# Value products of the samples' attention, ordered by page and turning over the four column quarters, in a two-layer decoder step

## The chip, the core and the metric

The kernel runs on one core of a Trainium2 chip. The metric is the device time of one execution in microseconds, as the median of the runs shown. TensorE multiplies and writes into PSUM, VectorE and ScalarE do elementwise work and empty PSUM, GpSimd (POOL) does elementwise work on SBUF and issues gathering DMAs, SyncE (SP) issues the other DMAs. Each engine works off its own queue in order, and semaphores tie the queues together.

## What is computed

The reference is one inference step of two decoder layers for a prompt of 512 tokens and for 8 samples, each with one new token and a paged cache of 2048 positions. A layer is a half-step FFN, a mixer and another half-step FFN, each with a LayerNorm. The mixer joins a state-space scan, a sparse attention and a short convolution. Only the sparse attention matters here. For a sample it has three branches (compressed keys, selected pages, window), each with its own softmax:

```python
s_c = einsum('btkgd,bnkd->btkgn', qg, kc);  o_c = softmax(s_c) @ vc          # 127 compressed positions
idx = top_k(score_from(p_c), 16)                                             # blocks of 64 positions
s_s = einsum('btkgd,btknsd->btkgns', qg, ks_sel);  o_s = softmax(s_s) @ vs_sel
s_w = einsum('btkgd,bwkd->btkgw', qg, kw);  o_w = softmax(s_w) @ vw          # last 512 positions
o = g[..., 0:1] * o_c + g[..., 1:2] * o_s + g[..., 2:3] * o_w
```

For the prompt the same three branches run over the 512 prompt tokens themselves. The compressed keys and values of a sample come from its whole cache by a small two-layer network (`nsa_compress`).

## The kernel before, in words

The products are 32-bit. The large ones are split into a high and a low half and run as three fast products; the small ones of the samples' attention run as plain 32-bit products, of which the profile shows each as two records (two weight loads, two matmuls).

The middle part of a layer (`mid`) has these stages. First, projections, and the fetch of the pages of the first group. Then `compress_cache`, a generator over the 8 samples: for each, eight steps of `prepare` (ScalarE and VectorE, L693 and L694, convert a slice of the 16 cache pages into two halves; the pages stand in tile cx or raw) and `products` (TensorE, L708, twelve matmuls), and then `second` (L736, L740). The pages of the next sample are fetched at the start of a sample (`fetch_cmp`, 16 DMAs on SP). `samples(l, g, ...)` is the attention of two samples, group g of four. Groups 0, 1 and 2 are woven with the compression of the next two samples, group 3 with `prompt_attention`, whose scores and values are L1048 to L1050, the transposes at L1060 and the values at L1071.

`weave` sets the order in which the two streams are written down: each stream yields the time that its last piece should cost, and the stream whose time has come goes next. So the numbers in `yield` are planned costs, in nanoseconds; a scheduler and the pools then place the instructions by engine.

In a group, z is the half of the pages (0 or 1) and j the sample (0 or 1). Page tile `G[z, j]` holds eight pages of keys (columns 0 to 127) and values (128 to 255) of one sample, in tile sg. Rows 64z + 32j to 64z + 32j + 31 of an output bank belong to (z, j): these 32 output rows are one column quarter of TensorE's array, so there are four quarters. `PT` holds the transposed probabilities, 128 columns for each of the eight page steps c and two window steps; `sT`, `srows` hold the new token's part (8 rows), `pc`, `vc` the compressed part (127 rows).

The value products at L1246 go through the quarters one by one: eight page steps of one quarter, with `fetch_sel` for that page tile of the next group behind them; for z = 0 the new token's product (L1250); a yield; two window steps (L1254); for z = 0 the new token's window product (L1257) and the compressed part (L1258). `fetch_sel` puts three gathering DMAs on POOL (L1111) and five DMAs on SP (L1115) for each page tile; they wait until the tile's value products have been read. `fetch_win` (L1120) loads two window tiles. Then three VectorE operations (L1262 to L1264) scale and add the branches, and L1266 sums on TensorE.

Of the kernel before, what the change touches and what calls it, by code (L numbers as in the profile page):

```python
# [122 lines left out]
class Trunk:  # L123
# [999 lines left out]
    def samples(self, l, g, p, pg, pw):  # L1123

        nc = self.nc
        G = self.sgq[g]
        QB, kcT, vc = self.QB, self.kcT, self.vc
# [18 lines left out]
        pc = p.tile([127, 64], F32, name="pc")  # L1146
# [3 lines left out]
        for k in range(4):  # L1150
            nc.tensor.matmul(M[:33, 196 + 33 * k:229 + 33 * k], pt[:, k:k + 1].to_broadcast([127, 33]), self.C["map"][:127],
                             start=True, stop=True)
        s, t = (p.tile([33, 4, 33], F32, name=n) for n in ("score", "rk"))
# [3 lines left out]
        own = p.tile([33, 4, 1], F32, name="own")  # L1157
# [17 lines left out]

        SB = p.tile([128, 1282], F32, name="SB")
        nc.vector.memset(SB[64:128, 0::1281], BIG)
        for c in range(2):
            S = self.bank(self.saS)
            for z in range(2):  # L1180
                for j in range(2):
                    r = 64 * z + 32 * j
                    nc.tensor.matmul(S[r:r + 32].rearrange("p (n t) -> p n t", n=4), QB[:, 2 * g + j], G[z, j][:, 4 * c:4 * c + 4, 0:128],
                                     start=True, stop=True)
                yield 1700.0, 0.0
            nc.vector.tensor_tensor(SB[:, 1 + 512 * c:513 + 512 * c].rearrange("p (n t) -> p n t", n=8), S.rearrange("p (n t) -> p n t", n=8),
                                    msk[:, 8 * c:8 * c + 8, None].to_broadcast([128, 8, 64]), op=OP.add)
        S = self.bank(self.saS)
        for j in range(2):
            for z in range(2):  # L1190
                r = 64 * z + 32 * j
# [26 lines left out]
        PT = p.tile([128, 10, 128], F32, name="PT")  # L1218
        for c0, n in ((0, 4), (4, 4), (8, 2)):
            T = self.bank(self.saT)  # L1220
            for c in range(n):
                o = 1 + 128 * (c0 + c)
                nc.tensor.transpose(T[:, c * 128:c * 128 + 128], SB[:, o:o + 128], self.ident)
            o, t = PT[:, c0:c0 + n].rearrange("p c r -> p (c r)"), T[:, :128 * n]
# [8 lines left out]
        sT = p.tile([NS, 128], F32, name="sT")  # L1233
# [4 lines left out]
        yield 300.0  # L1238

        O = self.bank(self.saS)  # L1240
        for z in range(2):
            for j in range(2):
                r = slice(64 * z + 32 * j, 64 * z + 32 * j + 32)
                own = slice(32 * j, 32 * j + 32)
                for c in range(8):
                    nc.tensor.matmul(O[r, :128], PT[:, c, r], G[z, j][:, c, 128:256], start=c == 0, stop=z == 1 and c == 7)  # L1246
                if g < 3:
                    self.fetch_sel(l, pg, g + 1, ((z, j),))
                if z == 0:
                    nc.tensor.matmul(O[r, :128], sT[:, own], self.srows[:, 128:256], start=False, stop=True)  # L1250
                yield 1900.0
                for c in range(2):
                    v = 512 + 256 * z + 128 * c
                    nc.tensor.matmul(O[r, 128:256], PT[:, 8 + c, r], G["w", j][:, v:v + 128], start=c == 0, stop=z == 1 and c == 1)  # L1254
                if z == 0:
                    o = slice(64 + 32 * j, 96 + 32 * j)
                    nc.tensor.matmul(O[r, 128:256], sT[:, o], self.srows[:, 384:512], start=False, stop=True)  # L1257
                    nc.tensor.matmul(O[r, 256:384], pc[:, own], vc[:127, j], start=True, stop=True)  # L1258
        if g < 3:
            self.fetch_win(l, pw, g + 1)  # L1260
        OS = p.tile([128, 128], F32, name="OS")
# [5 lines left out]
        for kv in range(2):  # L1267
            r = slice(kv * 64, kv * 64 + 64)
# [679 lines left out]
```

## Time and profile before

| | us |
|---|---|
| median of 3 runs | 3145.73 |
| lowest, highest | 3144.55, 3149.37 |
| profiled execution | 3151.41 |
| span of its trace, first to last instruction | 3149.70 |
| TensorE busy in it | 3078.8 |
| mean granted TensorE clock | 0.987 |

Terms of the sum are read from the one profiled execution, whose own time is 5.68 us above the median. In its trace the two layers repeat each other: the groups' value products begin at 555.7, 600.0, 648.9 and 703.3 us in the first layer. Busy time of TensorE counts a matmul to its modelled end, also where the next has begun, so differences of start times say more than durations.

### The profile page before, as it was taken

How to read it: one execution, taken by the hardware profiler on the slowest of the kernel's cores; microseconds unless marked ns; L12 is line 12 of the kernel's file. 1: busy time of each engine (PE TensorE's matmuls, PEld its weight loads, DVE VectorE, ACT ScalarE, POOL GpSimd, SP SyncE). 2: the span in 40 equal slices, each digit the busy share in tenths (PEclk: the TensorE clock that was granted, in tenths of full speed). 3: DMA queues.
4: the chain of work that ended last, by engine and by line, in shares of the span. 5: the costliest groups of instructions: out<-in, count | busy, mean ns of one | idle time of the engine just before them, and what ended most of it. 6: DMA issues, size and time to landing. Idle time of an engine off the chain costs nothing. (4 is left out here: it accounts for less than half of the span.)

```text
span 3149.7 us, 62116 instructions
## 1 busy us (share of the span) xinstructions
PE 3078.8 (98%) x25364; PEld 2949.6 (94%) x25364; DVE 1599.2 (51%) x3586; ACT 1121.1 (36%) x2226; POOL 531.5 (17%) x809
## 2 busy tenths in 40 slices
PE   8999999999999999999999999899999999999998
PEld 8999998877999999999999999888779999999998
DVE  7633356466655365333486334564566553653343
ACT  3332235455234233332233222254562242333322
POOL 2611031221001012001147110212210010210010
PEclk9999999999999999999999999899999999999999
DMA  5543254621543322223234332546215532322321
GB/s 156 202 149 133 89 152 136 205 81 29 173 131 106 96 86 96 93 82 100 76 117 170 99 101 83 162 123 213 68 54 165 136 105 81 108 81 85 104 84 65
DMA packets 358631, 360.18 MB, mean 114 GB/s; under 512 B 40069, under 2 KB 341669, under 8 KB 358217
## 3 DMA queue, kind: packets, MB, share of 16 engines
q1 hardware_dynamic: 342584, 333.58, 33.9%
q0 software_dynamic: 7440, 20.00, 2.2%
q8 instruction: 199, 3.26, 0.4%
q10 hardware_dynamic: 8320, 2.62, 0.4%
q14 instruction: 88, 0.71, 0.1%
HBM read 332.48 MB, written 36.28 MB: 117 GB/s over the span
## 5 line engine op out<-in xcount | busy, mean ns | idle before, releaser
L239 PE MATMUL ps<-xh,whi 128*128 128x264 f32 (+1 forms) x4448 | 1257.5, 285 | 15.3 <-ACT whi L228 7.8
L240 PE MATMUL ps<-xl,whi 128*128 128x264 f32 (+1 forms) x4448 | 1258.8, 284 | 2.0 <-DVE xl L323 2.0
L241 PE MATMUL ps<-xh,wlo 128*128 128x264 f32 (+1 forms) x4448 | 1255.5, 284 | 2.4 <-DVE wlo L229 2.4
L229 DVE TENSOR_TENSOR wlo<-raw,whi 128x1024 fp32r<-128x1024 f32 (+3 forms) x432 | 495.8, 1150 | 750.4 <-ACT whi L228 746.5
L239 PEld LDWEIGHTS ps<-xh,whi 128*128 128x128 f32 x4448 | 837.0, 189 | 20.1 <-ACT whi L228 8.8
L240 PEld LDWEIGHTS ps<-xl,whi 128*128 128x128 f32 x4448 | 840.1, 189 | 3.6 <-DVE xl L323 2.2
L241 PEld LDWEIGHTS ps<-xh,wlo 128*128 128x128 f32 x4448 | 839.6, 189 | 4.2 <-DVE wlo L229 3.6
L228 ACT ACTIVATE whi<-raw 128x1024 fp32r<-128x1024 f32 (+2 forms) x452 | 444.4, 988 | 892.2 <-PE ps L240 782.3
L240 PE MATMUL ps<-hl,whi 128*128 128x256 f32 (+1 forms) x1408 | 398.3, 283 | 0.0
L239 PE MATMUL ps<-hh,whi 128*128 128x256 f32 (+1 forms) x1408 | 398.2, 283 | 0.0
L241 PE MATMUL ps<-hh,wlo 128*128 128x256 f32 (+1 forms) x1408 | 398.1, 283 | 0.0
L241 PEld LDWEIGHTS ps<-hh,wlo 128*128 128x128 f32 x1408 | 265.3, 188 | 0.2
L239 PEld LDWEIGHTS ps<-hh,whi 128*128 128x128 f32 x1408 | 264.9, 188 | 0.3
L240 PEld LDWEIGHTS ps<-hl,whi 128*128 128x128 f32 x1408 | 264.8, 188 | 0.1
L260 POOL TENSOR_TENSOR xf<-xf,shift 128x264 f32<-128x264 f32 (+1 forms) x84 | 79.4, 982 | 1027.2 <-ACT shift L257 1027.2
L384 DVE TENSOR_TENSOR s<-s,ps 128x264 f32<-128x264 f32 (+1 forms) x176 | 74.3, 424 | 275.2 <-PE ps L241 274.9
L708 PE MATMUL ps<-xc,whi 128*128 128x256 f32 (+1 forms) x1024 | 165.2, 295 | 0.0
L385 ACT ACTIVATE hh<-s 128x264 fp32r<-128x264 f32 (+1 forms) x176 | 72.7, 415 | 245.7 <-DVE s L384 245.6
L708 PEld LDWEIGHTS ps<-xc,whi 128*128 128x128 f32 x1024 | 140.1, 190 | 14.6 <-issue 8.5
L1111 POOL DMA_INDIRECT sg<-in_selT_dram,idx x96 | 92.5, 963 | 289.9 <-PE ps L1246 257.3
L382 ACT ACTIVATE s<-ps 128x264 f32<-128x264 f32 (+1 forms) x176 | 66.2, 379 | 128.2 <-PE ps L241 126.0
L386 DVE TENSOR_TENSOR hl<-s,hh 128x264 fp32r<-128x264 f32 (+1 forms) x176 | 76.6, 437 | 33.5 <-ACT hh L385 33.5
(472 smaller groups left out, 4316.7 us busy)
## 6 DMA issues: line engine op xcount, KB each, us to landing
raw<-in_ffn_w_gu_dram SPq DMA_DIRECT2D x86, 1024.0 KB
raw<-in_w_in_dram SPq DMA_DIRECT2D x38, 1024.0 KB
raw<-in_ffn_w_down_dram SPq DMA_DIRECT2D x32, 1024.0 KB
sg<-in_selT_dram SPq DMA_DIRECT2D x160, 128.0 KB
cx<-in_cmpT_dram SPq DMA_DIRECT2D x128, 128.0 KB
raw<-in_cmpT_dram SPq DMA_DIRECT2D x128, 128.0 KB
raw<-in_ffn_w_down_dram SPq DMA_DIRECT2D x16, 768.0 KB
W<-in_winT_dram SPq DMA_DIRECT2D x16, 512.0 KB
```

Source lines behind the costliest of these rows:

```text
L228: self.copy = self.nc.scalar.activation(hi, raw, AF.Copy)
L229: self.lo.tensor_sub(lo, raw, hi.bitcast(F32))
L239: nc.tensor.matmul(o, hi[:, k], rh, start=start and k == 0, stop=False)
L240: nc.tensor.matmul(o, hi[:, k], rl, start=False, stop=False)
L241: nc.tensor.matmul(o, lo[:, k], rh, start=False, stop=stop and k == nk - 1)
L260: nc.gpsimd.tensor_sub(self.xf[:, g, a:b], self.xf[:, g, a:b], sc[:, :n])
L382: nc.scalar.activation(s[:, :n], g, AF.Silu)
L384: nc.vector.tensor_mul(s[:, :n], s[:, :n], u)
L385: nc.scalar.activation(hh[:, j, a:b], s[:, :n], AF.Copy)
L386: nc.vector.tensor_sub(hl[:, j, a:b], s[:, :n], hh[:, j, a:b].bitcast(F32))
L708: nc.tensor.matmul(o, w[:, 2 * qq + q2, :], x[:, 2 * q2:2 * q2 + 2, z:z + n], start=not b and s < 2 and q2 + z + m == 0, stop=s > 5 and q2 ...
L1111: nc.gpsimd.indirect_dma_start(out=t[:, k], out_offset=None, in_=flat, in_offset=bass.IndirectOffsetOnAxis(ap=self.idx[:, l, b, z, k:k + 1 ...
```

## The change

The value products of a group are written in another order. The page steps c are now the outer loop, and inside a step the four quarters take turns; the two window steps likewise. After page steps 3 and 7 the generator yields. `fetch_sel` is called once, for all four page tiles, behind the last page step. The products of the new token and of the compressed part come last, for one sample and then the other. Since the parts of a quarter now share its bank without finishing one after the other, only the very first product in a quarter starts the sum anew, and the check of groups is switched off for these products. The score products keep their order of quarters and yield once for four products (2200 planned ns) in place of twice (1700 each).

```diff
+        quarters = [(z, j, slice(64 * z + 32 * j, 64 * z + 32 * j + 32)) for z in range(2) for j in range(2)]
         for c in range(2):
             S = self.bank(self.saS)
-            for z in range(2):
-                for j in range(2):
-                    r = 64 * z + 32 * j
-                    nc.tensor.matmul(S[r:r + 32].rearrange("p (n t) -> p n t", n=4), QB[:, 2 * g + j], G[z, j][:, 4 * c:4 * c + 4, 0:128],
-                                     start=True, stop=True)
-                yield 1700.0, 0.0
+            for z, j, r in quarters:
+                nc.tensor.matmul(S[r].rearrange("p (n t) -> p n t", n=4), QB[:, 2 * g + j], G[z, j][:, 4 * c:4 * c + 4, 0:128],
+                                 start=True, stop=True)
+            yield 2200.0, 0.0
...
         O = self.bank(self.saS)
-        for z in range(2):
-            for j in range(2):
-                r = slice(64 * z + 32 * j, 64 * z + 32 * j + 32)
-                own = slice(32 * j, 32 * j + 32)
-                for c in range(8):
-                    nc.tensor.matmul(O[r, :128], PT[:, c, r], G[z, j][:, c, 128:256], start=c == 0, stop=z == 1 and c == 7)
-                if g < 3:
-                    self.fetch_sel(l, pg, g + 1, ((z, j),))
-                if z == 0:
-                    nc.tensor.matmul(O[r, :128], sT[:, own], self.srows[:, 128:256], start=False, stop=True)
+        for c in range(8):
+            for z, j, r in quarters:
+                nc.tensor.matmul(O[r, :128], PT[:, c, r], G[z, j][:, c, 128:256], start=c == 0, stop=z == 1 and c == 7,
+                                 skip_group_check=True)
+            if c % 4 == 3:
                 yield 1900.0
-                for c in range(2):
-                    v = 512 + 256 * z + 128 * c
-                    nc.tensor.matmul(O[r, 128:256], PT[:, 8 + c, r], G["w", j][:, v:v + 128], start=c == 0, stop=z == 1 and c == 1)
-                if z == 0:
-                    o = slice(64 + 32 * j, 96 + 32 * j)
-                    nc.tensor.matmul(O[r, 128:256], sT[:, o], self.srows[:, 384:512], start=False, stop=True)
-                    nc.tensor.matmul(O[r, 256:384], pc[:, own], vc[:127, j], start=True, stop=True)
+        if g < 3:
+            self.fetch_sel(l, pg, g + 1)
+        for c in range(2):
+            for z, j, r in quarters:
+                v = 512 + 256 * z + 128 * c
+                nc.tensor.matmul(O[r, 128:256], PT[:, 8 + c, r], G["w", j][:, v:v + 128], start=False, stop=z == 1 and c == 1,
+                                 skip_group_check=True)
+        for j in range(2):
+            own, o = slice(32 * j, 32 * j + 32), slice(64 + 32 * j, 96 + 32 * j)
+            nc.tensor.matmul(O[own, :128], sT[:, own], self.srows[:, 128:256], start=False, stop=True, skip_group_check=True)
+            nc.tensor.matmul(O[own, 128:256], sT[:, o], self.srows[:, 384:512], start=False, stop=True, skip_group_check=True)
+            nc.tensor.matmul(O[own, 256:384], pc[:, own], vc[:127, j], start=False, stop=True, skip_group_check=True)
+        yield 900.0
```

On TensorE's queue, in the first group of the first layer, the value products stood like this before (sg_5104, sg_5124, sg_5144 and sg_5164 are the page tiles of the four quarters; x8 is eight products in a row):

```order
L1246 MATMUL ps_6737<-sg_5104,PT_6595 32x128 x8
L1250 MATMUL ps_6737<-srows_4762,sT_6716 32x128
L1254 MATMUL ps_6737<-W_5184,PT_6595 32x128 x2
L1257 MATMUL ps_6737<-srows_4762,sT_6716 32x128
L1258 MATMUL ps_6737<-vc_6088,pc_6427 32x128
L1246 MATMUL ps_6737<-sg_5124,PT_6595 32x128 x8
L1250 MATMUL ps_6737<-srows_4762,sT_6716 32x128
```

Now the same place begins as follows, and goes on so for 32 products:

```order
L1242 MATMUL ps_6737<-sg_5104,PT_6595 32x128
L1242 MATMUL ps_6737<-sg_5124,PT_6595 32x128
L1242 MATMUL ps_6737<-sg_5144,PT_6595 32x128
L1242 MATMUL ps_6737<-sg_5164,PT_6595 32x128
L1242 MATMUL ps_6737<-sg_5104,PT_6595 32x128
```

The quarter changes with every product, where it changed after eight products and the small ones behind them.

In the second group of the first layer the compression (L708) cuts in. The beginning of the group's value products on TensorE's queue, before (-) and now (+):

```order
 L708 MATMUL ps<-xc_5864,whi 128x256 x4
-L1246 MATMUL ps<-sg,PT 32x128 x7
-L1250 MATMUL ps<-srows,sT 32x128
+L1242 MATMUL ps<-sg,PT 32x128 x15
 L708 MATMUL ps<-xc_5861,whi 128x256 x4
 L708 MATMUL ps<-xc_5861,wlo 128x256 x4
 L708 MATMUL ps<-xc_5862,whi 128x256 x4
-L1254 MATMUL ps<-W,PT 32x128 x2
-L1257 MATMUL ps<-srows,sT 32x128
-L1258 MATMUL ps<-vc,pc 32x128
-L1246 MATMUL ps<-sg,PT 32x128 x8
-L1250 MATMUL ps<-srows,sT 32x128
```

Ahead of this piece one value product stands alone in both. Now 15 and 16 follow, with twelve L708 products between, and the page values of the group are through two interruptions earlier.

The closing part of the same group on TensorE's queue, now:

```order
L1251 MATMUL ps<-W,PT 32x128 x8
L1255 MATMUL ps<-srows,sT 32x128
L1256 MATMUL ps<-srows,sT 32x128
L1257 MATMUL ps<-vc,pc 32x128
L1255 MATMUL ps<-srows,sT 32x128
L1256 MATMUL ps<-srows,sT 32x128
L1257 MATMUL ps<-vc,pc 32x128
```

The window products, which stood in four pairs, are one row of eight, and the two 8-row products of a sample stand together. In the first groups the 32 page products stand in one row (x32); in the fourth groups, beside the prompt's attention, they stand as 5, 11 and 16. The rows of SP and POOL are the same in both kernels.

## Rows read from the trace of the kernel before

**Rows 1.** The page's first part: busy us, share of the span, instructions, by engine.
```profile
PE 3078.8 (98%) x25364; PEld 2949.6 (94%) x25364; DVE 1599.2 (51%) x3586; ACT 1121.1 (36%) x2226; POOL 531.5 (17%) x809
```

**Rows 2.** Stretches: length, busy us of PE, PEld, DVE, ACT, POOL; clock, DMA share, GB/s.
```profile
555.00:574.00 19.00, 19.00 (x162) 15.87 (x161) 5.69 (x19) 6.13 (x13) 11.56 (x12) 1.00 0.71 209
...
730.00:790.00 60.00, 58.69 (x517) 44.56 (x516) 40.36 (x76) 38.41 (x97) 8.22 (x7) 1.00 0.10 28
...
673.70:680.50 6.80, 5.94 (x33) 5.32 (x33) 4.29 (x21) 2.98 (x12) 1.04 (x1) 0.53 0.03 10
```

**Rows 3.** Waits from 495 to 683: waiter, released by: us, times, longest.
```profile
ACT xc L693 <- PE ps L708: 69.6, 39, 5.7
```

**Rows 4.** TensorE's instructions by line and shape: count, busy us, mean ns, idle.
```profile
L1246 PE MATMUL ps<-sg,PT 128*32 128x128 f32 x512 | 62.6, 274 | 0.0
...
L1254 PE MATMUL ps<-W,PT 128*32 128x128 f32 x128 | 20.0, 279 | 0.0
```

**Rows 5.** TensorE in time order, first group: start us, us, line, records (x).
```profile
555.71 1.94 PE L1246 MATMUL ps<-sg,PT 128*32 128x128 f32 x16
557.57 0.40 PE L1250 MATMUL ps<-srows,sT 8*32 8x128 f32 x2
557.90 0.62 PE L1254 MATMUL ps<-W,PT 128*32 128x128 f32 x4
...
560.99 0.74 PE L708 MATMUL ps<-xc,whi 128*128 128x256 f32 x4
...
562.61 0.62 PE L1254 MATMUL ps<-W,PT 128*32 128x128 f32 x4
...
565.37 0.74 PE L708 MATMUL ps<-xc,whi 128*128 128x256 f32 x4
...
567.00 0.30 PE L1254 MATMUL ps<-W,PT 128*32 128x128 f32 x1
567.01 0.30 PE L1246 MATMUL ps<-sg,PT 128*32 128x128 f32 x1
...
568.88 0.75 PE L708 MATMUL ps<-xc,whi 128*128 128x256 f32 x4
...
570.51 0.62 PE L1254 MATMUL ps<-W,PT 128*32 128x128 f32 x4
571.07 0.75 PE L708 MATMUL ps<-xc,whi 128*128 128x256 f32 x4
```

**Rows 6.** TensorE in time order, two other stages.
```profile
157.97 0.67 PE L1505 MATMUL ps<-room 128*32 128x128 f32 x16
158.56 0.39 PE L239 MATMUL ps<-xh,whi 128*128 128x264 f32 x1
...
778.22 1.09 PE L1071 MATMUL ps<-wlo,rows 128*64 128x128 f32 x16
779.25 0.50 PE L1048 MATMUL ps<-ks,raw 128*128 128x512 f32 x1
```

**Rows 7.** Fetches: POOL and SP in time order, landing times, busy time by stretch.
```profile
571.96 0.99 POOL L1111 DMA_INDIRECT sg<-in_selT_dram,idx  x1 [0.30 <-issue]
...
573.48 11.44 SPq L641 DMA_DIRECT2D raw<-in_cmpT_dram  x16
...
DMA to landing us min/median/max: 2.6/3.6/5.4
...
558.00:572.00 14.00, 14.00 (x117) 11.80 (x118) 2.27 (x5) 3.20 (x5) 10.53 (x12) 1.00 0.83 245
572.00:586.00 14.00, 14.00 (x109) 10.40 (x108) 8.02 (x28) 5.88 (x13) 0.94 (x1) 1.00 0.89 281
```

**Rows 8.** In time order: second group's scores on TensorE, ScalarE's conversions of fetched pages.
```profile
582.33 1.23 PE L1183 MATMUL ps<-sg,QB 128*32 128x512 f32 x8
...
587.61 0.42 ACT L693 ACTIVATE xc<-raw 128x256 fp32r<-128x256 f32 x1 [0.80 <-PE ps L708]
589.55 0.42 ACT L693 ACTIVATE xc<-raw 128x256 fp32r<-128x256 f32 x1 [1.52 <-PE ps L708]
```

## The prediction

> **What bounds the kernel now.** I read the page first. TensorE is busy for 98% of the span, VectorE for half of it, ScalarE for a third [rows 1]; since matmuls are pipelined and their ends are modelled, that says which engine to look at and not yet that it is the bound. So I read the busy time by stretch next, around the samples' attention. In the first group's value products (555 to 574 us) TensorE is busy for all of 19 us, and in the prompt attention that follows the last group it is busy for 58.69 of 60 us [rows 2]. Then the waits between 495 and 683 us, where three groups run beside the compression of the cache: ScalarE's conversions wait for TensorE's L708 products 39 times, 69.6 us in all [rows 3]. There TensorE is what the others wait for, so a microsecond taken off its queue is a microsecond off the kernel until something else is late. The two layers show the same stretches, so all is worked out for one layer and doubled.
>
> **What a group costs now.** One 32-bit product is two records in the trace. A group holds 64 records of page values (L1246), 16 of window values (L1254) and 12 of the new token and the compressed part; the first two are the 512 and 128 of [rows 4], over 2 layers and 4 groups. In time order, in the first group [rows 5]: sixteen L1246 records, all in one 32-column quarter, take 557.57 - 555.71 = 1.86 us up to the next instruction; four L1254 records in one quarter take 571.07 - 570.51 = 0.56. So a record costs (1.86 - 0.56) / 12 = 0.108 us, and a change to products of another shape about 0.2 us on top: the two L1250 records, which use 8 rows, take 557.90 - 557.57 = 0.33. The four stretches of the group are 5.28 (555.71 to 560.99), 2.76 (562.61 to 565.37), 1.88 (567.00 to 568.88) and 0.56: 10.5 us of TensorE's time. The other groups hold the same records, cut up a little differently; I take 10.5 to 10.6 for each.
>
> **What turning over the quarters costs.** The trace has products of this shape in all four quarters of one bank, in another stage (L1505): sixteen records take 158.56 - 157.97 = 0.59 us [rows 6], against 1.86 in one quarter. That is what four records in one quarter take, plus 0.03: the quarters run side by side. The kernel before shows it for the value products too: from 567.00 on, four L1254 records of one quarter run beside sixteen L1246 of another, and the whole takes 1.88, as sixteen alone do [rows 5]. So n records by turns cost 0.59 + 0.108 x (n - 16) / 4: 1.89 us for 64, 1.02 for 32, 0.97 for 30, 0.75 for 22, 0.43 for 10, 0.33 for 2.
> The closing part of a group then is: 16 window records 0.59; the four 8-row records of one sample, now together, 0.33 + 2 x 0.108 = 0.55; the two of the compressed part 0.33; and both again for the other sample: 2.35 us.
> Groups as they now stand on the queue: first, 64 in a row, 1.89 + 2.35 = 4.24; second and third, 2 + 30 + 32 records, 2.32 + 2.35 = 4.67; fourth, 10 + 22 + 32, 2.20 + 2.35 = 4.55. Each stretch also costs about 0.1 us where it is entered, and there are two fewer in the first, second and fourth group, one fewer in the third. Saved: 6.4, 6.1, 5.9 and 6.2 us, 24.6 a layer, **49.2 us** for both.
>
> The score products (128 columns of keys each) already go by turns over the quarters in the kernel before and stand in the same order after; only their planned cost changes, which I cost at nothing: the neighbours of these products on the queue are the same. The DMAs of SP and POOL keep their order. What moves is when they are let go.
>
> **Who is late next.** (a) The next group's pages. Before, each of the four page tiles was fetched as soon as its quarter was through; now all four wait for the thirty-second product, which comes about when the first quarter came before (some 1.9 us after the first product). POOL's twelve fetches run one after the other in both kernels, from the first release on; the last starts at 571.96, and they land 3.6 us after issue in the median, 5.4 at most [rows 7]: 575.6 to 577.4. The next scores stand at 582.33 [rows 8]; 6.4 us earlier is 575.9. So 0 to 1.5 us of stall after the first group; I take 0.6. (b) The compressed cache. Behind its 20 page fetches SP issues two window fetches and 16 pages of the next compression, until 573.48 + 11.44 = 584.9 [rows 7]. From 558 to 586 the DMA engines are busy for 0.83 and 0.89 of 14 us each, 24.1 us of full use [rows 7]; at 0.95, from 558, that ends at 583.4. ScalarE reads these pages at 587.61 [rows 8], then 581.2: 2.2 us late, of which 1.52 are idle before ScalarE's next conversion anyway [rows 8]. 0 to 2.2, and I take 0.7. After the second group 0.3, after the third none, since the compression is over. (c) Chains over ScalarE and VectorE that a shorter queue covers less: today's nearest row is the 1.3 us that TensorE sits idle in 60 of prompt attention [rows 2]; I take that once more, 1.3 us a layer, between 0 and 3. Together 2.9 us a layer, 5.8 in all.
> **Sum:** 49.2 - 5.8 = 43.4 us. The profiled execution took 3151.41 us (3149.70 of span), the median of three is 3145.73. On the median: **3102**; a profiled execution should come out near 3108.
>
> **Rivals.** The forecast with its small losses: 3094 to 3110.
> *The fetches become the bound.* If the page and cache transfers can't be pressed together at all, the first group keeps only its slack: the pages are in by 586 and read at 587.61 [rows 7, 8], about 1.6 us; the second I treat alike. A layer then loses (6.4 - 1.6) + (6.1 - 1.6) = 9.3, and the 1.3 of (c): 21.2 us in both, so 28 are won: 3118. For it: 0.89 of the engines are in use already. Against: in 558 to 572 the use is 0.83, because fetches wait for quarters.
> *TensorE's supply runs dry.* L1505 shows sixteen records, no row shows sixty-four. The closest longer row is that of L1071: sixteen records over two halves in 779.25 - 778.22 = 1.03 us [rows 6]. If records behind the sixteenth of a batch came at that spacing, 0.054 us instead of 0.027, the first group would lose 48 x 0.027 = 1.3 us, the others about 30 x 0.027 = 0.8: 3.7 a layer, 7.4 in all: 3109.
> The Trainium skill, in "TensorE: Matmul & The Clock Gate", Part 1, section on 56 against 53.3 ns, says that with hardware decoding off the sequencer spends about 62 ns per matmul. By that, an estimate, the 80 records by turns take 5.0 us a group instead of 2.5, and the time would be some 20 us longer, 3122; the sixteen records in 0.59 us come faster than that, but they may have been queued, so no row settles it.
> *Nothing is lost:* 49.2 us, 3097. *The clock:* a stretch at half clock stands between the groups and the prompt attention (0.53 from 673.7 to 680.5, where TensorE was busy for 5.94 of 6.80 us) [rows 2]. If it goes, 3.4 us a layer are won; if one more comes, 3.4 are lost.
> *Slower:* a change of quarter inside an accumulation costs what a change of shape costs. Then each of the 40 products of a group takes 0.33 us, as the two L1250 records do [rows 5]: 13.2 us and 1.8 for the rest, 15.0 against 10.5, 36 us in all: 3182. It turns to a loss above 0.22 us a product. Against it stand the sixteen records in 0.59 us, eight products of 0.07 each.
> *No change:* TensorE is not the bound where it looks so, or the planner's new costs place work so that the gaps take up the gain: 3146. The waits for L708 speak against that.
>
> **How the numbers follow.** Forecast 0.56; nothing lost 0.10; supply 0.09; fetches 0.18; slower 0.04; no change 0.03. About 0.2%, 6 us, is what a measurement of this kernel can tell from no change. Faster by more: 0.93, within: 0.03, slower: 0.04. The range goes from 3092 (nothing lost and one stretch of half clock gone) to 3119 (the fetches): it leaves out the slower case, no change, half a stretch more on each side, and the supply by the page's figure.
>
> **What would show it.** In the profile after: the 64 value records of the first group end within 2.0 us of their start, and TensorE's time in the products of a group falls from 10.5 to about 4.5 us: the first step is right. Waits of TensorE's score products for page fetches, or of ScalarE's conversions for the compressed pages: the fetches take part of it, and the scores that stood at 582.33 come less than 6 us earlier, counted from the first group's first value product. If the stretch at half clock moves or doubles, the sum is off by 3.4 us for each. The forecast fails if value records by turns start more than 0.05 us apart, or if the time of a group does not follow that of its products.

## The result, and the profile after

The changed kernel took 3112.49 us in the median of four runs (3106.87 to 3114.33), the kernel before 3145.14 beside it: a ratio of 0.9889, 95% interval 0.9872 to 0.9907. A second time it was 3112.51 against 3146.18 (0.9911, 0.9885 to 0.9937). The forecast was 3102 in a range of 3092 to 3119. The sign and the range held; of the 43 us that were forecast, 33 came. So the question is where 10 us went.

TensorE in time order, first group of the first layer (start us, us, line, records), answers to [rows 5]:

```profile
553.11 1.96 PE L1242 MATMUL ps<-sg,PT 128*32 128x128 f32 x64
554.99 0.74 PE L708 MATMUL ps<-xc,whi 128*128 128x256 f32 x4
...
556.62 0.64 PE L1251 MATMUL ps<-W,PT 128*32 128x128 f32 x16
557.20 0.40 PE L1255 MATMUL ps<-srows,sT 8*32 8x128 f32 x2
...
558.63 0.41 PE L1257 MATMUL ps<-vc,pc 127*32 127x128 f32 x2
558.97 0.39 PE L708 MATMUL ps<-xc,whi 128*128 128x256 f32 x1
```

The 64 page records take 554.99 - 553.11 = 1.88 us, the closing part 558.97 - 556.62 = 2.35. The group that held TensorE for 10.48 us in [rows 5] holds it for 4.23.

Whether the time follows is read from instructions that stand in both traces in the same place: an instruction's start before minus its start after is what has been won up to it. TensorE, first layer, three of its lines in the kernel before:

```profile
553.99 1.09 PE L1223 MATMUL ps<-cst,SB 128*128 128x128 f32 x8
581.86 0.38 PE L1142 MATMUL ps<-cst,scp 64*127 64x4 f32 x2
598.36 1.03 PE L1223 MATMUL ps<-cst,SB 128*128 128x128 f32 x8
629.56 0.38 PE L1142 MATMUL ps<-cst,scp 64*127 64x4 f32 x2
742.37 0.87 PE L1071 MATMUL ps<-wlo,rows 128*64 128x128 f32 x10
```

And the same instructions after (L1223 is L1222 there):

```profile
551.39 1.09 PE L1222 MATMUL ps<-cst,SB 128*128 128x128 f32 x8
572.76 0.38 PE L1142 MATMUL ps<-cst,scp 64*127 64x4 f32 x2
591.94 1.04 PE L1222 MATMUL ps<-cst,SB 128*128 128x128 f32 x8
616.99 0.38 PE L1142 MATMUL ps<-cst,scp 64*127 64x4 f32 x2
721.12 0.87 PE L1071 MATMUL ps<-wlo,rows 128*64 128x128 f32 x10
```

The differences are 2.60, 9.10, 6.42, 12.57 and 21.25. The first 2.6 were won ahead of the attention. From the first group's transposes to the next group's scores 6.5 us are won (forecast 6.4), in the second group 12.57 - 6.42 = 6.15 (forecast 6.1). But between, from L1142 to the transposes behind the scores, 9.10 - 6.42 = 2.7 are given back. The second group gives back 1.3, read up to the transposes of L1203 (L1202 after), where the difference is 11.31. The whole attention of the first layer wins 21.25 - 2.60 = 18.7 us. In the second layer the differences at the same six places are 26.02, 32.53, 27.34, 33.49, 30.01 and 40.73 at the end: it wins 6.5, gives back 5.2, wins 6.2, gives back 3.5, and ends at 14.7. That is 33.4 in all, against 43.4 forecast.

The place where it is given back, TensorE in the second group's scores, first layer and then second layer (in brackets: idle before, and what ended it):

```profile
573.23 1.05 PE L1182 MATMUL ps<-sg,QB 128*32 128x512 f32 x4
576.15 1.14 PE L1182 MATMUL ps<-sg,QB 128*32 128x512 f32 x4 [1.86 <-DMA raw<-in_cmpT_dram]
...
2116.61 1.05 PE L1182 MATMUL ps<-sg,QB 128*32 128x512 f32 x4
2120.53 1.12 PE L1182 MATMUL ps<-sg,QB 128*32 128x512 f32 x4 [2.87 <-DMA sg<-in_selT_dram,idx]
```

Three of the four tiles are there; the products of the fourth wait. The row of before shows no such wait [rows 8]. TensorE's waits in the three groups, first layer (553 to 690 us) and then second layer (2096 to 2240), in total, times, longest:

```profile
PE ps L1182 <- DMA raw<-in_cmpT_dram: 1.9, 1, 1.9
PE ps L1182 <- DMA W<-in_winT_dram: 1.1, 1, 1.1
...
PE ps L1182 <- DMA sg<-in_selT_dram,idx: 4.6, 2, 2.9
```

L1182 reads only page tiles, so the names `raw` and `W` can't be right; the section on the prediction shows from the DMA packets which transfer it was. Together 7.6 us. Part of the rest is the clock (stretch, busy us of PE, PEld, DVE, ACT, POOL, clock, DMA share, GB/s; first group of the first layer, first and second group of the second):

```profile
553.11:593.60 40.49, 37.72 (x353) 30.10 (x353) 20.92 (x68) 19.90 (x42) 12.04 (x12) 1.00 0.75 232
...
2096.49:2139.51 43.02, 39.17 (x354) 30.66 (x353) 20.92 (x68) 19.91 (x42) 12.05 (x12) 0.96 0.72 221
2139.51:2185.12 45.61, 42.88 (x376) 33.24 (x375) 22.43 (x72) 21.35 (x46) 12.05 (x12) 0.96 0.54 163
```

In the second layer a stretch of 3.4 us at half clock (1.2 GHz) follows each of the two waits, behind idle times of 2.87 and 1.70 us, and costs some 1.7 us, half its length. In the first layer (idle 1.86 and 1.07 us), and in the second run of this kernel (1.7 to 2.1 us each time), the stretches behind the waits are absent.

### The profile page after: what moved, and what is told of

Read it like the earlier page. It is cut to its first block, busy times and chain, and to the rows that moved or that the text cites. A ratio compares the mean times of both kernels' runs of the same rounds, so it can differ in the third digit from the quotient of the medians.

```text
span 3110.9 us, 62132 instructions
## 1 busy us (share of the span) xinstructions
PE 3037.4 (98%) x25364; PEld 2908.1 (93%) x25364; DVE 1599.5 (51%) x3586; ACT 1121.8 (36%) x2226; POOL 538.6 (17%) x809
## 5 line engine op out<-in xcount | busy, mean ns | idle before, releaser
L239 PE MATMUL ps<-xh,whi 128*128 128x264 f32 (+1 forms) x4448 | 1258.0, 286 | 14.4 <-ACT whi L228 6.9
L708 PE MATMUL ps<-xc,whi 128*128 128x256 f32 (+1 forms) x1024 | 166.2, 296 | 0.1
L708 PEld LDWEIGHTS ps<-xc,whi 128*128 128x128 f32 x1024 | 141.0, 191 | 14.9 <-issue 8.9
```

What stands on the lines that cost most here:

```text
L239: nc.tensor.matmul(o, hi[:, k], rh, start=start and k == 0, stop=False)
L708: nc.tensor.matmul(o, w[:, 2 * qq + q2, :], x[:, 2 * q2:2 * q2 + 2, z:z + n], start=not b and s < 2 and q2 + z + m == 0, stop=s > 5 and q2 ...
```

## The experiments

Three chips were met. On the first the kernel before, timed beside the others, takes 3144 to 3146 us; a_sp ran on another one, alike in this. On the one called the second below, where it takes 3172, four kernels ran. "Won in the attention" is the reading above, of both layers, against the profiled run of the kernel before; 33.4 (18.7 + 14.7) for the changed kernel.

**A quarter's pages taken away (a_3q).**

```diff
-            self.fetch_sel(l, pg, g + 1)
+            self.fetch_sel(l, pg, g + 1, ((0, 0), (0, 1), (1, 0)))
+            self.sgq[g + 1][1, 1] = self.sgq[g + 1][1, 0]
```

> The changed kernel, with the pages of the quarter (1, 1) not fetched from the second group on: its products read the tile of quarter (1, 0) instead. 24 page transfers a group in place of 32; no engine's instructions change in number. Left out: those page contents, so the output differs. Theory (in the first and second group the change has made the next group's page transfers the last to arrive, and the scores wait for them): the transfers end some 5 us earlier, the score products wait under 0.5 us where they now wait 1.9 to 2.9, and the attention of both layers together loses about 11 of the 13 us it now loses there: 3098 to 3104 us. Rival (the losses at the scores come from the order of TensorE's queue or from chains over ScalarE and VectorE): 3110 to 3115.

Measured: 3101.63, ratio 0.9873 (0.9857 to 0.989). TensorE in the second group's scores:

```profile
572.61 1.05 PE L1182 MATMUL ps<-sg,QB 128*32 128x512 f32 x2
...
574.05 1.07 PE L1182 MATMUL ps<-sg,QB 128*32 128x512 f32 x8
...
575.43 1.06 PE L1182 MATMUL ps<-sg,QB 128*32 128x512 f32 x6
```

No wait. 21.5 and 24.9 us are won in the attention, 46.4 in all: 13 more than with all pages, as the theory has it. With four buffers for three tiles one tile of the group after next can also go early, so this is a little more than a quarter less. The 13 us aren't the transfers' alone, since the planner also placed the second and third groups' page products as 32 and 32 in place of 2, 30 and 32. That the waits come from the page transfers is plain here; regs2_again below, whose products stand as in the changed kernel, shows it with all pages.

**One more gather for each quarter on POOL (a_ng4).**

```diff
-NG = 3
+NG = 4
```

> The changed kernel with four of a quarter's eight pages gathered by POOL and four fetched by SP, in place of three and five: POOL issues 16 DMAs a group, SP 16. The bytes are the same. If the page transfers are limited by the DMA engines (0.85 of them in use after the release): POOL's last issue comes 5 us later but SP's pages land earlier, and the time stays within 4 us of the changed kernel: 3109 to 3117. If they are limited by the issuing queue: POOL's sixteen issues at 1.25 us take 20 us instead of 15, the last page lands 5 us later in the first and second group of each layer, and the time is 3125 to 3133.

Measured: 3117.41 (0.9916, 0.99 to 0.9933): by the time the first case, by the trace the second. POOL's last gather, TensorE's score products, and its waits in the first layer:

```profile
574.89 0.94 POOL L1111 DMA_INDIRECT sg<-in_selT_dram,idx  x1 [0.30 <-issue]
...
574.91 1.04 PE L1182 MATMUL ps<-sg,QB 128*32 128x512 f32 x2 [1.15 <-DMA sg<-in_selT_dram,idx]
579.16 2.12 PE L1182 MATMUL ps<-sg,QB 128*32 128x512 f32 x4 [3.20 <-DMA sg<-in_selT_dram,idx]
...
PE ps L1182 <- DMA sg<-in_selT_dram,idx: 8.4, 4, 3.2
```

The last gather is issued 22.3 us after the group's first value product (16.4 in the changed kernel), SP's last page already after 11.5; the waits grow to 8.4 and 9.1 us a layer, and the attention wins only 5.8 and 5.4. That is 22 us less. The waits are 10 of it; the half-clock stretches within the attention, 48 us in place of 17, can be 15 more. The time is only 5 longer: between the layers this run was 10 us ahead of the changed kernel's profile, with 17 us of half clock there against 31. The page products stand as in a_3q, so the order differs here too. So the time alone would have led astray; the waits say that the issuing queue counts.

**The fetch written later (b_late).**

```diff
-                if g < 3:
-                    self.fetch_sel(l, pg, g + 1, ((z, j),))
+                if g < 3 and z == 1 and j == 1:
+                    self.fetch_sel(l, pg, g + 1)
```

> The kernel before, with the fetch of the next group's pages written behind the fourth quarter's page products instead of behind each quarter's own: all four tiles are let go together, some 11 us later than the first is now. Nothing else changes. Theory (from the release the pages need 21 to 22 us): the scores, which stand 25 us behind the group's first value product, wait for about 8 us in the first and second group of each layer, nothing in the third: 3145 + 4 x 8 = 3177, between 3168 and 3185. Rival (slack elsewhere hides the transfers): 3143 to 3150.

Measured: 3144.86 (1.0004, 0.9995 to 1.0014). POOL's first gather:

```profile
558.50 0.96 POOL L1111 DMA_INDIRECT sg<-in_selT_dram,idx  x1 [66.10 <-PE ps L1246]
```

It starts as early as before. The transfer waits for the last reader of the buffer that it overwrites, not for the place where it is written, so the edit moved nothing, and the expectation was wrong about what it does. It says something on the change, though: what releases the tiles later is the turning itself, which puts each quarter's last product into the last turn.

**Only the closing part of the change (b_close).** Its first new lines, against the kernel before:

```diff
+        for z, j, r in quarters:
+            for c in range(8):
+                nc.tensor.matmul(O[r, :128], PT[:, c, r], G[z, j][:, c, 128:256], start=c == 0, stop=z == 1 and c == 7,
+                                 skip_group_check=True)
+            if g < 3:
+                self.fetch_sel(l, pg, g + 1, ((z, j),))
+            yield 1900.0
...
```

> The kernel before with only the closing part of the change: the page products stay one quarter after the other, each quarter's tile released behind its own; the window products go by turns over the quarters and the 8-row products stand together, behind them all. From the records: the page products then take about 7.2 us of TensorE's time a group, the closing part 2.34, 9.5 in all against 10.5, and one more stretch is entered: 0.8 us less a group, 6 to 8 us less in all, 3137 to 3140. The rest of the gain is the page products' own turning. Rival (the closing part carries half of the gain, since its switches of shape cost more than the records show): 3128 to 3132.

Measured: 3136.86 (0.9978, 0.9969 to 0.9988), 5.2 us won in the attention of each layer. In the first group the page products take 3.20 + 1.87 + 1.87, the closing part 2.34: 9.28 us against 10.48. So about 8 of the 33 us, by the medians, are the closing part's. The rest comes with turning the page products and the scores' new planned cost, which stayed as before here; no run takes these two apart.

**The same bytes issued faster (regs2_again), with an earlier release too (both_again), and the changed kernel beside them (after_again).** The first edit:

```diff
-NG = 3
+NG = 2
...
+        rows = self.pages(src, l, slice(2 * g, 2 * g + 2), 0, 16)
...
-            for k, s in enumerate(self.pages(src, l, b, 8 * z + NG, 8 - NG)):
-                nc.sync.dma_start(t[:, NG + k], s)
+            for k in range(NG, 8):
+                nc.sync.dma_start(t[:, k], rows[16 * j + 8 * z + k])
```

The second, in both_again alone:

```diff
-        yield 300.0
+        yield 300.0, 0.0
...
-            if c % 4 == 3:
-                yield 1900.0
+            if c == 7:
+                yield 3800.0
```

> The changed kernel itself. On the chip of the first runs (kernel before 3144.5) it should take 3109 to 3115 again. On a chip like that of the last four runs, where the kernel before takes 3172, two near relatives of the changed kernel were slower than it by 0.8 and 0.9%: there it should take 3185 to 3202, and its trace should show TensorE standing idle behind the first group's products for no wait that has a transfer at its end, while POOL issues its gathers and SP's issues stand 1.4 us apart instead of 0.5.

> The changed kernel with the faster issue (one load of page numbers ahead of the fetches, POOL gathers 8 pages a group, SP 24). On the chip of the first runs: 3102 to 3107 if the issuing queues set when the last page arrives, 3110 to 3115 if the DMA engines do. On a chip where the kernel before takes 3172: 3164 to 3173, as measured there.

> The changed kernel with the faster issue and the earlier release. On the chip of the first runs: 3098 to 3105 if queue and release set when the last page arrives, 3106 to 3112 if the DMA engines do. On a chip where the kernel before takes 3172: 3153 to 3162, as measured there.

Measured on the first chip: 3112.51, 3105.11 (0.9875, 0.9851 to 0.9899) and 3104.94 (0.9872, 0.9855 to 0.9888). SP, POOL's last gather and TensorE's scores in regs2_again, whose group starts at 555.9:

```profile
557.90 13.07 SPq L1116 DMA_DIRECT2D sg<-in_selT_dram  x24
...
567.33 0.95 POOL L1112 DMA_INDIRECT sg<-in_selT_dram,idx  x1 [0.30 <-issue]
...
576.04 1.17 PE L1183 MATMUL ps<-sg,QB 128*32 128x512 f32 x8
```

SP's last page is issued 14.7 us after the first value product (16.7 in the changed kernel), POOL's 11.4 (16.4), and no score product waits for a page in either layer. The bytes are the same and come in time, so it wasn't the number of bytes that held the scores up in the changed kernel, but that the last pages went out too late. In the attention 18.9 and 19.7 us are won, 5 more than in the changed kernel, which is less than the waits alone: the half-clock stretches within the attention, 17 us in the changed kernel, come to 31, and the third group wins 0.5 and 0.8 us where it won 4.5 and 5.3. The earlier release adds nothing that can be measured, since no page is late any more. Both medians are some 7 us below the changed kernel's. The intervals of the three ratios just touch or overlap, so as a better version they are likely and not proved; that the waits are gone is plain in the trace. This run moves SP's issues and POOL's gathers at once; which of them came last in the changed kernel, its own packets tell (below).

**All pages on SP (a_sp).** The edit against regs2_again:

```diff
-            for k in range(NG):
-                nc.gpsimd.indirect_dma_start(
...
-            for k in range(NG, 8):
+            for k in range(8):
```

> The changed kernel with the page numbers read in one load and all 32 page transfers of a group issued by SP: no gathers on POOL. The bytes are the same. SP's last issue comes 32 x 0.52 = 16.6 us after the first. On the chip where the kernel before takes 3144: if the length of the issuing queue sets the end of the train, the scores of the second and third group wait for 1 to 2 us each, less than in the changed kernel and more than with 24 issues on SP, 3107 to 3112; if it was the gathers on POOL alone that came late (6.6 us from the last issue to the scores' start), SP's transfers land sooner and nothing waits: 3103 to 3107. On a chip like the second one, where the kernel before takes 3172: if POOL's gathers are what holds up SP's issues and TensorE's signals there, the stalls go and the time comes to 3105 to 3140; if the stalls come with any dense train of transfers, 3155 to 3175.

Measured beside a kernel before of 3145.84: 3127.54 (0.9937, 0.9919 to 0.9956), outside what was expected. SP's train, and TensorE's waits in the first layer:

```profile
563.52 18.17 SPq L1112 DMA_DIRECT2D sg<-in_selT_dram  x32
...
PE ps L1219 <- ACT SB L1207: 5.7, 2, 2.9
PE ps L1199 <- DVE mx L1197: 1.7, 2, 1.0
```

No page wait; the time went into the chain of the softmax instead (TensorE's transposes wait for ScalarE's exponentials, 5.7 us a layer). The planner, which counts the gathers, had placed the last score product and the compression's work otherwise. So this run doesn't tell how fast SP alone is; that the planner's other placing is what made the chain wait is likely and not shown.

**On the second chip (a_regs2, a_early, a_pairs, a_both).** a_regs2 and a_both are the kernels of regs2_again and both_again. a_early has the second edit alone. a_pairs turns over two quarters at a time:

```diff
-        for c in range(8):
-            for z, j, r in quarters:
...
+        for z in range(2):
+            for c in range(8):
+                for _, j, r in quarters[2 * z:2 * z + 2]:
...
+            if g < 3:
+                self.fetch_sel(l, pg, g + 1, ((z, 0), (z, 1)))
+            yield 1900.0
```

> The changed kernel with the same page transfers issued faster: SP reads a group's page numbers in one load ahead of the fetches, where it now reads them four times, 1.2 us before each quarter; and POOL gathers two of a quarter's eight pages (8 DMAs a group), SP fetches six (24). SP's last issue then comes 24 x 0.52 = 12.5 us after the release instead of 15, POOL's after 10 instead of 15. The bytes are the same. If the issuing queues set the end of the train: the waits of the scores in the first and second group of each layer (1.9 to 2.9 us) fall under 1 us, and the time comes to 3102 to 3107. If the DMA engines set it (0.85 in use): the waits stay, 3110 to 3115.

> The changed kernel with the second, third and fourth group's 32 page products in one row on TensorE, as the first group has them: the planner is given one pause of 3800 behind them in place of two of 1900, and none ahead of them. The second group's tiles are then let go some 3.5 us earlier on TensorE's queue, measured from the group's first value product, and 24 L708 products more stand between them and the next scores. Theory (release to arrival is what the scores wait for): the wait at the third group's scores goes (1.1 to 1.6 us in the first layer, 3.8 in the second), that at the second group's scores stays: 3105 to 3109. Rival (the wait has another cause): 3111 to 3115.

> The changed kernel with the page products by turns over two quarters only, first the two of z = 0, then the two of z = 1, each pair's tiles let go behind its products; the closing part as in the change. From the records at two quarters (0.054 us) the 64 page records take about 3.5 us instead of 1.88: 1.6 us more of TensorE's time a group. Theory (in the first and second group the page transfers arrive last, so TensorE's time ahead of them is worth nothing): only the third and fourth group pay, 2 x 2 x 1.6 = 6.5 us, 3117 to 3121. If all groups pay: 8 x 1.6 = 13 us, 3124 to 3128.

> The changed kernel with the edits of the faster issue and of the earlier release together. If queue and release set the end of the page train, the scores wait nowhere over 0.5 us, and the time comes near that of the run with three quarters' pages (3102): 3098 to 3105. If the DMA engines set it: 3106 to 3112.

Measured: 3168.61 (0.9992, 0.998 to 1.0003), 3200.31 (1.0091, 1.0076 to 1.0107), 3197.0 (1.0082, 1.0064 to 1.0099) and 3160.65 (0.9958, 0.9945 to 0.9972), against 3172.32 for the kernel before. All four expectations were written for the first chip and are missed. The trace of a_early, first group: SP's page issues, TensorE, ScalarE, then the longest waits from 555 to 600 us:

```profile
560.66 21.55 SPq L1115 DMA_DIRECT2D sg<-in_selT_dram  x20
...
568.60 1.05 PE L708 MATMUL ps<-xc,whi 128*128 128x256 f32 x4
572.36 0.75 PE L708 MATMUL ps<-xc,whi 128*128 128x256 f32 x4 [2.71 <-issue]
...
571.58 0.72 ACT L693 ACTIVATE xc<-raw 128x256 fp32r<-128x256 f32 x2 [12.09 <-remote]
...
ACT xc L693 <- remote: 17.8, 2, 12.1
DVE xc L694 <- remote: 11.7, 1, 11.7
```

While POOL gathers (560.91 to 575.6), SP's twenty issues take 21.55 us instead of 15.05, and signals arrive late: the last of TensorE's L708 products ends at 569.65, ScalarE, which waits for a count that the profile names only as remote, TensorE's as far as can be seen, goes on at 571.58, and TensorE then waits for ScalarE. The half clock comes on top (0.975 over the span). a_early and a_both differ only in the faster issue with its eight gathers, and by 40 us. The changed kernel itself wasn't timed on this chip, and of the kernel before there is no trace there: that its 28 us more than on the first chip have the same cause, and what delays the signals, stays open. So does the question for which a_pairs was made.

## Why the prediction was right, and where it was off

**What bounds the kernel.** Right: a group's TensorE time fell by 6.2, 5.9, 5.8 and 5.9 us, and up to the next scores 6.5 and 6.15 us were won in the first and second group of both layers, where 6.4 and 6.1 were forecast.

**The price of turning.** Right to 0.01 us: 1.89 forecast and 1.88 measured for 64 records, 2.35 and 2.35 for the closing part. The sixteen records of another stage [rows 6] were a good enough row: sixty-four in a row keep 0.029 us each. (For few records the formula was too low: for two it gives 0.21 and not the 0.33 that stands beside it, and 0.34 was measured; ten took 0.55 against 0.43.) That settles two rivals. The supply doesn't run dry, and a change of quarter costs nothing like a change of shape. A third rival is gone as well: 64 records take 1.88 us, 29 ns each, also far behind the sixteenth; a product, two records, takes 59. The figure that it went by, about 62 ns a matmul, is given by the Trainium skill ("TensorE: Matmul & The Clock Gate", Part 1, the section on 56 against 53.3 ns) for hardware decoding off. Read as the price of a record it isn't met here, and whether decoding was off no run shows.

**Term (a), the next group's pages, is the one that was mis-sized.** The forecast had 0.6 us a layer there, and 0.3 for the second group with its cache pages. The two groups gave back 2.7 + 1.3 = 4.0 us in the first layer and 5.2 + 3.5 = 8.7 in the second (2.5 + 2.2 and 2.9 + 2.2 in the second run); of the 8.7 some 3.4 us are the half clock behind the waits.

Two steps failed. First, the arrival: I took the last gather's start and added the landing times of a table, 3.6 to 5.4. POOL's last issue came about where I put it, 16.4 us behind the first value product, but the scores went on 6.6 us later in the first layer and 7.6 in the second; the landing times of [rows 7] are those of the gathers that the trace could follow, five of twelve in the first group's train, and the last was not among them. The packets of the DMA queues date it all the same (q0 is POOL's queue: 48 packets for each gather in every run; q1 is SP's).

Queue rows of the changed kernel from 574.00 to 575.56 us and from 575.56 to 590, then of the kernel before from 577.00 to 578.74 and from 578.74 to 590; where no q0 stands, POOL's queue moves nothing more:

```profile
q0 software_dynamic: 10, 0.02, 3.8%
...
q1 hardware_dynamic: 3473, 3.25, 72.3%
...
q0 software_dynamic: 34, 0.07, 11.5%
...
q1 hardware_dynamic: 2425, 2.22, 65.3%
```

The last gather's last packet ends at 575.55, and the score products go on at 576.15. So it is in the other three waits (619.21 and 619.58, 2120.09 and 2120.53, 2165.54 and 2166.11) and in all four of the second run, whatever transfer the profile names; by the count of its packets SP's twentieth page is in 1.2 to 3.4 us earlier each time. So the last to land was POOL's last gather, 5.5 to 7.2 us behind its issue. In the kernel before it had landed at 578.73, 6.8 us behind its issue and not 5.4 at most, and nothing waited for it. With that landing the prediction's own sum, scores at 575.9, gives 2.8 us of stall, and 2.7 were measured. Why it lands so late is open in part. Busy time by stretch from its issue to its landing (DMA share 0.91):

```profile
569.52:575.55 6.03, 4.76 (x29) 2.81 (x27) 2.52 (x8) 2.73 (x6) 1.19 (x1) 1.00 0.91 296
```

The engines then also move SP's window and cache transfers; yet in a_ng4, where they are at 0.86, the last gather lands 3.7 us behind its issue.

Second, the release in the second group. "About when the first quarter came before" was worked out for the first group, whose 64 records stand in a row. The second group's stand as 2, 30 and 32 with the compression's products between, which the order had shown. SP's trains in the second group, before and then after:

```profile
603.73 16.04 SPq L1115 DMA_DIRECT2D sg<-in_selT_dram  x20
...
599.31 15.19 SPq L1115 DMA_DIRECT2D sg<-in_selT_dram  x20
```

Against the group's first product (600.02 and 593.60) that is 3.7 us before and 5.7 after: two microseconds later, towards scores that come six earlier.

**Term (b), the compressed cache:** nothing was lost that can be seen. ScalarE's conversions wait 1.1 and 1.6 us a layer for these pages (none and 1.6 before), and none of TensorE's L708 products waits for a conversion. **Term (c), the chains:** 1.3 a layer forecast; the third and fourth group won 9.9 and 10.7 us of 12.1, so 2.2 and 1.4 were lost, inside the stated 0 to 3. The 1.4 had help: the half-clock stretch there is 3.4 us shorter than before.

**The rivals.** "The fetches become the bound" was given 0.18 and 3118, and it is the mechanism that took the 10 us. It was priced by the use of the DMA engines, 0.83 and 0.89 [rows 7]; regs2_again shows that the same bytes can be in time, and with a_ng4 that the issuing queues set when the last page starts out. How long it then takes, with the engines at 0.87 to 0.91, is a part of the loss that no run separates. "Nothing is lost" (3097) is some 4 us below what a_3q gives (3101.63) with the waits gone. The clock moved by a few us both ways, as was said.

**The median.** The profiled spans differ by 38.8 us, the medians by 33. The 5 us more were won outside the attention, where the two profiles differ by 6 us of half clock; the profile of before also took 6 us more than the median. That the attention's own 33.4 agrees with the medians is in part luck: it holds the two half-clock stretches behind the waits, and the second run, which lacks them, won 36.3 there.

## What to carry to other kernels

When a queue gets shorter, date the last transfer of the next stage from its release to its use, group by group, and not from a table of landing times: here a train of 32 transfers took 20 to 22 us from release to use, of which the issuing queue was 14.4 and the last gather's landing 5.5 to 7.2. Before turning products that read several buffers, ask when each buffer is let go: turning releases all of them last. Small column-tiled products of one shape should go by turns over the quarters of the array; that was worth 5 of 7 us a group here, and its price could be read from another stage of the same trace.

## What the runs showed of the hardware that was not expected

- Reading page numbers costs SP 1.2 us each time, while its page issues stand 0.52 us apart; one load for a whole group, ahead of the release, took 2 us off the train even with four issues more.
- Two chips differ by 28 us for the kernel before, and in the sign for relatives of the change: 1.009 for one on the second chip, where in the place shown ScalarE went on 1.9 us after the product that it waited for, while POOL gathered.
- Half-clock stretches fell elsewhere with every edit: 86 us of them in the profile before, 83 after. In a_ng4 they were 31 us longer within the attention than in the changed kernel and 14 us shorter between the layers.
- A gather on POOL's queue landed 2.4 to 7.2 us behind its issue, by the packets of the last one of each train, where the table of landing times, which holds a part of them only, ends at 5.4.
